# Two of eight depthwise convolution blocks on column strips of TensorE, and 64-partition transposes around the triangular inverses, in a one-layer RWKV-7 and Conformer trunk

## The chip, the core and the metric

The kernel runs on one core of one Trainium2 chip. The engines named below are those of the core: PE (TensorE, matrix products), DVE (VectorE), ACT (ScalarE), POOL (GpSimd) and SP (SyncE), which issues all DMA transfers of this kernel. PE reads its operands from SBUF, an on-chip memory of 128 partitions, and writes its results to banks of PSUM. Each engine executes its own instructions strictly in order, and waits at an instruction until the semaphores that it needs have been raised by other engines or by transfers.

The metric is the device time of one execution in microseconds (us): the median over several runs.

## The reference

One layer is computed for 1024 tokens of width 1024, in float32. A token mixer has two groups of channels that share an input projection and an output projection: an RWKV-7 recurrence with 8 heads of 64, and a causal depthwise convolution over 512 channels with 31 taps behind a gated unit. A feed-forward part with a small convolution follows.

```python
def _causal_dwconv(x, w, b):          # x: (B, T, C), w: (31, C)
    ...
    y = lax.conv_general_dilated(x, w[:, None, :], window_strides=(1,), padding=((K - 1, 0),),
                                 feature_group_count=x.shape[-1], ...)
    return y + b
...
def _wkv7(r, decay, k, v, a_vec, b_vec):
    def step(S, inp):
        sa = jnp.einsum("bhvk,bhk->bhv", S, a_t)
        S = S * w_t[:, :, None, :] + sa[..., None] * b_t[:, :, None, :] + v_t[..., None] * k_t[:, :, None, :]
        y = jnp.einsum("bhvk,bhk->bhv", S, r_t)
...
    c = u[..., :D_CONV] * jax.nn.sigmoid(u[..., D_CONV:])
    c = _causal_dwconv(c, cconv_w, cconv_b)
    c = jax.nn.silu(_layer_norm(c, cln_g, cln_b))
    mix = jnp.concatenate([rwkv_out, c], axis=-1) @ w_out
...
    x = x + _rms_norm(mix, norm_post_mix)
    f = _conv_ffn(_rms_norm(x, norm_pre_ffn), ffn_up, ffn_conv_w, ffn_conv_b, ffn_down)
    x = x + _rms_norm(f, norm_post_ffn)
```

The reference steps through the recurrence token by token. The kernel works it in chunks of 64 tokens, which needs, for each chunk and head, the inverse of a triangular 64x64 matrix.

## The kernel before

**Tiling.** The 1024 tokens are two halves of 512 (`h`), four quarters of 256 (`q`, two in each half), and sixteen chunks of 64 tokens, four in a quarter. A quarter thus has 4 chunks x 8 heads = 32 triangular matrices, held side by side. Channels lie in blocks of 128 on the partitions.

**Projections.** A weight tile is loaded by SP into `wr` (3 buffers, L159), split into a high and a low part (L153: the high part `wh` on ACT, the low part `wl` on POOL, 2 buffers each), and PE forms three products for each tile of the contraction into a PSUM bank `pb` (L126). This is so for the input projection `w_in`, for `w_out` and for the feed-forward part.

**The convolution group.** `glu_in` makes a tile `c` of 128 channels with 30 tokens of history ahead of 512 tokens. `conv` (L363 to L373) convolves it: one ACT instruction writes tap 0 and the bias into the PSUM bank `pc` (L370), and 30 dependent DVE instructions add the other taps (L373), the last of them into the SBUF tile `co`. There are four blocks of channels for each of two halves, so eight calls; they are written (half, block). The bank `pc` exists once and is shared with `conv_norm`, which normalizes the four `co` tiles of a half.

**The recurrence.** For a quarter, DVE and ACT work through elementwise decays, PE forms the scores (L473 to L498), and DVE scales them (`keys`, L500 to L520) into a tile `l` of 128 partitions x 32 matrices x 64 tokens. `inverses` (L532 to L551) then inverts the four 16x16 diagonal blocks of each of the 32 matrices by substitution: four transposes on DVE, each on 32 partitions (L539), bring them into the tile `dw`, and 14 pairs of small dependent DVE operations (`sub` at L549, `dw` at L551) work through the rows. `merge` (from L553) transposes the result back (two transposes at L561, four at L566, each on 32 partitions) and joins the 16x16 inverses into 64x64 ones by small products on PE (16 to 32 rows) with copies by ACT between them. The first PE instruction of a merge reads `dw`, so it is a good landmark: "merge q2" is the merge of quarter 2. After the merge the chunks of the quarter go through the recurrence proper in sequence (L643 to L686).

**What sets the order.** Every piece of work belongs to a stream ("first", "top", "rwkv", "norm", "conv", "proj"), and each stream has a number in the table `PRIO`. A scheduler takes these priorities, the dependencies and the buffers that are free, and writes out a fixed order for each engine ahead of time. The recurrence stands ahead of `norm`, `conv` and `proj`, which fill what it leaves. A call `conv(h, i, behind)` may only be scheduled behind a given instruction. In `mixer` (from L992) the calls (1,0) and (1,1) stand behind `sts[0]["normed"]` (the last instruction of the first half's `conv_norm`), (1,2) behind `W[3].mark` (the last transpose of quarter 3's merge), and (1,3) follows it. The order of the second half is: convolutions (1,0) and (1,1), output projection `w_out(0)` of the first half, quarter 3, `norm_ffn(0)`, convolutions (1,2) and (1,3), and then the feed-forward part.

Of the kernel before, what the change touches and what calls it, by code (L numbers as in the profile page):

```python
# [22 lines left out]
P = 128  # L23
# [13 lines left out]
CONV_W = 31  # L37
D_FF = 2816
# [8 lines left out]
BUFS = {"v": 2, "gd": 1, "pt": 6, "kk": 1, "l8": 5, "ca": 6, "ck": 6, "r": 2,  # L47
        "mixr": 1, "co": 4, "po": 1, "c": 4, "t2": 2}
EARLY, EVERY = 8, 3

# [41 lines left out]
class Trunk:  # L92
# [252 lines left out]
    def glu_in(self, h, hs, st, i):  # L345
# [3 lines left out]
        c = self.tl("c", [P, CONV_W - 1 + HALF])  # L349
        with self.tc.high_priority():  # L350
            nc.scalar.activation(c[:, CONV_W - 1:], ps2, AF.Tanh, scale=0.5)
# [5 lines left out]
        with self.tc.high_priority():  # L357
            nc.vector.scalar_tensor_tensor(c[:, CONV_W - 1:], c[:, CONV_W - 1:], 1.0, ps1, ALU.add, ALU.mult)
        if h == 0:
            nc.gpsimd.tensor_copy(self.ccarry[:, i], c[:, HALF:])  # L360
# [3 lines left out]
    def conv(self, st, i):  # L364
# [6 lines left out]
        for j in range(1, CONV_W):  # L371
            out = co if j == CONV_W - 1 else acc
            nc.vector.scalar_tensor_tensor(out, c[:, j:j + HALF], w(j), acc, ALU.mult, ALU.add)  # L373

# [125 lines left out]
    def keys(self, w):  # L500
# [14 lines left out]
        nc.gpsimd.memset(RT[32:64, :, 0:32], 0.0)  # L515
# [16 lines left out]
    def inverses(self, w):  # L532
# [3 lines left out]
        for g in range(2):  # L536
            for e in range(2):
                o = 16 * (1 - e)
                nc.vector.transpose(  # L539
                    self.dw[64 * e + 32 * g:64 * e + 32 * g + 32, o:o + 512].rearrange("p (i j) -> p i j", i=16),  # L540
                    Lq[64 + 32 * g:96 + 32 * g, :, 32 * g + 16 * e:32 * g + 16 * e + 16].rearrange("p u t -> p t u"))
# [11 lines left out]
    def merge(self, w):  # L553
# [5 lines left out]
        for g in range(2):  # L559
            gs = slice(32 * g, 32 * g + 32)  # L560
            nc.vector.transpose(up[gs].rearrange("p u j -> p j u"),  # L561
                                self.dw[gs, 16:1040].rearrange("p (i j) -> p j i", j=32)[:, 0:16])
            for e in range(2):
                o = 16 * (1 - e)
                c = 32 * g + 16 * e
                w.mark = nc.vector.transpose(  # L566
                    RT[gs, :, c:c + 16].rearrange("p u i -> p i u"),
                    self.dw[64 * e + 32 * g:64 * e + 32 * g + 32, o:o + 512].rearrange("p (i j) -> p i j", i=16))
# [378 lines left out]
    def mixer(self, sts):  # L947
# [60 lines left out]
        def conv(h, i, behind=None):  # L1008

            with ExitStack() as gate, self.stream("conv"):  # L1010
# [149 lines left out]
```

## Time and profile before

| | |
|---|---|
| median of 3 runs | 1372.5 us (1372.45 to 1373.0) |
| the profiled execution | 1373.94 us |
| its span in the profile | 1372.2 us |
| mean granted TensorE clock | 0.971 |
| instructions | 22752 |
| DVE busy in the span | 777.1 us |
| ACT busy in the span | 658.1 us |
| POOL busy in the span | 571.4 us |

The profile takes one execution apart. The execution lasted 1.7 us more than its span, which begins with the first instruction and ends with the last. "Busy" is the time in which an engine executes something. Consecutive matrix products overlap in PE, and the length that the profile gives to one is longer than the distance from one to the next, so a PE that is busy need not be at its peak. The chain of waits follows back from the last instruction to what released it at each step.

Some moments of this execution, each the start of an instruction in the timeline of PE, serve as landmarks below:

| landmark | us |
|---|---|
| merge q0 begins on PE | 139.8 |
| first score of quarter 2 | 343.2 |
| merge q2 begins on PE | 428.0 |
| first score of quarter 3 | 482.3 |
| merge q3 begins on PE | 523.9 |
| first product of the feed-forward part | 556.6 |

### The profile page before, as it was taken

Reading aid. Unit: us, or ns where it says so; the run is one execution under the profiler, and the core shown is the slowest. Engines: PE = TensorE matmul, PEld = TensorE weight load, DVE = VectorE, ACT = ScalarE, POOL = GpSimd, SP = SyncE. Lnnn points to the kernel's source line nnn. Section 1 sums busy time; section 2 is a strip of 40 time slices with the busy share of each in tenths; the row PEclk is TensorE's granted clock in tenths of the full one; section 3 lists DMA queues with packets and bytes.
Section 4 is the critical chain, followed back from the end, with each engine's and each line's share of the span. In section 5 each row is a group of like instructions: output and inputs, shape, how many; then the busy total and the mean of one; then the engine's idle time right before and its main releaser. Section 6 shows DMA issues by size and latency. Waiting matters only on the chain.

```text
span 1372.2 us, 22752 instructions
## 1 busy us (share of the span) xinstructions
PE 1299.9 (95%) x8688; PEld 1055.0 (77%) x8688; DVE 777.1 (57%) x1354; ACT 658.1 (48%) x1307; POOL 571.4 (42%) x496
## 2 busy tenths in 40 slices
PE   5999989999987996999999999999999999999998
PEld 4766767687776875878798888788888888888886
DVE  5367998997799969996315445500036654441002
ACT  6562553556645745647535555522244444443222
POOL 4443322243441331345444554444444544544443
PEclk9999889999998996999999999999999999999999
DMA  6222111121211423123345443443335443333333
GB/s 208 84 74 70 53 42 33 50 67 54 61 59 58 145 78 116 40 70 93 99 133 164 125 133 121 147 128 92 94 99 155 129 131 94 99 96 97 92 93 114
DMA packets 72252, 133.49 MB, mean 97 GB/s; under 512 B 7792, under 2 KB 14320, under 8 KB 72144
## 3 DMA queue, kind: packets, MB, share of 16 engines
q1 hardware_dynamic: 72144, 132.05, 32.6%
q8 instruction: 68, 1.11, 0.3%
q14 instruction: 40, 0.33, 0.1%
HBM read 119.43 MB, written 12.58 MB: 96 GB/s over the span
## 4 chain that ended last, share of the span: by engine, by line
PE 73%; DVE 18%; ACT 4%; issue 3%; DMA 1%; POOL 1%; SPq 0%; POOLq 0%; DVEq 0%; ACTq 0%
PE pb L126 65%; DVE pc L373 5%; PE pe L126 4%; PE xs L126 1%; DVE l L566 1%; DVE sub L549 1%; DVE dw L539 1%; DVE dw L551 1%; POOL wl L153 1%; DVE pt L442 1%; DVE l L506 1%; PE pe L141 1%; DVE dw L561 1%; PE Y L126 0%; DMA l<-x 0%
## 5 line engine op out<-in xcount | busy, mean ns | idle before, releaser
L153 POOL TENSOR_TENSOR wl<-wr,wh 128x512 fp32r<-128x512 f32 x376 | 495.1, 1318 | 622.5 <-ACT wh L153 599.7
L153 ACT CAST wh<-wr 128x512 fp32r<-128x512 f32 x376 | 231.5, 616 | 461.3 <-PE pb L126 263.3
L126 PE MATMUL pb<-f,wh 128*128 128x512 f32 x1408 | 436.9, 391 | 3.4 <-ACT pb L746 1.9
L126 PEld LDWEIGHTS pb<-f,wh 128*128 128x128 f32 x1408 | 264.0, 188 | 58.4 <-ACT pb L746 2.1
L126 PE MATMUL pb<-f,wl 128*128 128x512 f32 x704 | 276.4, 393 | 1.2 <-POOL wl L153 1.2
L126 PE MATMUL pb<-h,wh 128*128 128x512 f32 (+2 forms) x704 | 231.4, 407 | 2.6 <-ACT wh L153 2.3
L850 DVE SCALAR_TENSOR_TENSOR acc<-pb,params,acc 128x511 f32<-128x511 f32 (+1 forms) x144 | 107.5, 747 | 163.5 <-ACT acc L845 97.9
L373 DVE SCALAR_TENSOR_TENSOR pc<-c,params,pc 128x512 f32<-128x512 f32 x232 | 174.0, 750 | 6.5 <-ACT pc L370 3.1
L126 PEld LDWEIGHTS pb<-h,wh 128*128 128x128 f32 (+2 forms) x704 | 129.6, 188 | 37.0 <-ACT wh L153 4.4
L126 PEld LDWEIGHTS pb<-f,wl 128*128 128x128 f32 x704 | 132.4, 188 | 29.6 <-POOL wl L153 2.0
L126 PE MATMUL pb<-h,wl 128*128 128x512 f32 (+2 forms) x352 | 144.1, 409 | 2.5 <-POOL wl L153 2.5
L903 DVE TENSOR_TENSOR row<-pb,post_ffn 128x512 f32<-128x512 f32 x16 | 10.2, 685 | 209.2 <-ACT junk L902 209.2
L126 PE MATMUL pb<-wl,ahi 128*128 128x512 f32 x320 | 126.9, 397 | 0.1
L126 PE MATMUL pb<-wh,alo 128*128 128x512 f32 x320 | 126.2, 394 | 0.0
L126 PE MATMUL pb<-wh,ahi 128*128 128x512 f32 x320 | 88.6, 396 | 0.0
L126 PEld LDWEIGHTS pb<-h,wl 128*128 128x128 f32 (+2 forms) x352 | 66.0, 187 | 20.4 <-POOL wl L153 4.0
L126 PEld LDWEIGHTS pb<-wl,ahi 128*128 128x128 f32 x320 | 60.1, 188 | 14.9 <-POOL wl L153 0.6
L126 PEld LDWEIGHTS pb<-wh,alo 128*128 128x128 f32 x320 | 60.1, 188 | 14.4
L126 PEld LDWEIGHTS pb<-wh,ahi 128*128 128x128 f32 x320 | 59.7, 188 | 14.6
L126 PE MATMUL pb<-wh,m 128*128 128x256 f32 x256 | 52.5, 299 | 3.8 <-ACT m L153 2.9
L845 ACT ACTIVATE acc<-pb,params 128x512 f32<-128x512 f32 x72 | 55.7, 774 | 0.0
L153 DVE TENSOR_TENSOR alo<-acc,ahi 128x512 fp32r<-128x512 f32 x36 | 35.4, 983 | 24.9 <-ACT ahi L153 24.9
(248 smaller groups left out, 1807.8 us busy)
## 6 DMA issues: line engine op xcount, KB each, us to landing
wr<-ffn_up SPq DMA_DIRECT2D x176, 256.0 KB, 2.7
wr<-ffn_down SPq DMA_DIRECT2D x88, 256.0 KB, 2.7
wr<-w_in SPq DMA_DIRECT2D x80, 256.0 KB, 2.7
wr<-w_out SPq DMA_DIRECT2D x32, 256.0 KB, 2.7
mixd<-t SPq DMA_DIRECT2D x16, 256.0 KB, 3.1
nrow<-x1d SPq DMA_DIRECT2D x8, 512.0 KB, 4.2
out<-nrow SPq DMA_DIRECT2D x16, 256.0 KB, 2.4
l<-x SPq DMA_DIRECT2D x8, 256.0 KB, 5.7
```

Of the source, the lines that this page charges most:

```text
L126: return self.nc.tensor.matmul(out, lhsT, rhs, start=start, stop=stop, skip_group_check=skip)
L141: self.nc.tensor.transpose(out, in_, self.con("ident")[:n, :n])
L153: return self.nc.scalar.copy(hi, src), eng.tensor_tensor(lo, src, hi.bitcast(F32), ALU.subtract)
L373: nc.vector.scalar_tensor_tensor(out, c[:, j:j + HALF], w(j), acc, ALU.mult, ALU.add)
L442: nc.vector.tensor_tensor_scan(sg[:, l], self.con("scan"), sg[:, l], 0.0, ALU.mult, ALU.add)
L506: nc.vector.tensor_tensor(bv, bv, ge, ALU.mult)
L539: nc.vector.transpose(self.dw[64 * e + 32 * g:64 * e + 32 * g + 32, o:o + 512].rearrange("p (i j) -> p i j", i=16), Lq[64 + 32 * g:96 + 32 ...
L549: nc.vector.tensor_tensor(tv, dv[:, j + 1:, j:j + 1].broadcast_to([P, n, j]), dv[:, j:j + 1, :j].broadcast_to([P, n, j]), ALU.mult)
L551: nc.vector.tensor_tensor(dv[:, j + 1:, :j], dv[:, j + 1:, :j], tv, ALU.add)
L561: nc.vector.transpose(up[gs].rearrange("p u j -> p j u"), self.dw[gs, 16:1040].rearrange("p (i j) -> p j i", j=32)[:, 0:16])
L845: nc.scalar.activation(acc, ps, AF.Identity, scale=w(2), bias=self.par("fb", ch))
L850: nc.vector.scalar_tensor_tensor(acc[:, o:], ps[:, :HALF - o], w(j), acc[:, o:], ALU.mult, ALU.add)
```

## The change

The change has three parts; line numbers after it are higher by 4 (in the helpers at the top of the file) to 32 and more.

**Strips.** Convolutions (1,0) and (1,1) become `conv_strips`. `glu_in` writes the tile `c`, with two more columns of zeros, to a buffer `cd` in DRAM. `conv_strips` loads a tile of taps `cw` (128 x 1024 floats, from a new input that holds diagonal 32x32 blocks of taps), and for each of four blocks of 128 tokens reads `cd` back four times, shifted by 0 to 3 tokens, into `cs`: 4 shifts x 32 channels on the partitions, with the four groups of 32 channels side by side. Eight rounds of matmuls (4 taps each, 32 with one zero tap) then accumulate into `pc`; in a round four matmuls, one for each group of 32 channels, write 32 partitions each, from 32 columns of PE. That is 128 matmuls for a convolution, chained so that they keep their order. One ACT instruction writes `co`. `cs` and `cw` have one buffer each. `c` goes from 4 buffers to 2, and `ca` (masked scores of the recurrence) from 6 to 5.

**Transposes.** Two transposes on 64 partitions take the place of the four on 32 in `inverses`, three of the six in `merge`. A transpose moves blocks of 32x32, so some blocks must be moved along the free dimension besides: ACT copies one of 32x32x32 ahead of the first transposes and one behind the last, and a POOL memset of the tile `RT` moves from `keys` to behind the last transposes.

**Order.** (1,0) and (1,1) have no gate any more, (1,2) stands ahead of `w_out(0)` behind `W[2].mark`, and (1,3) stands behind `W[3].mark`.

```diff
@@ constants
-BUFS = {... "ca": 6, ... "c": 4, "t2": 2}
+BUFS = {... "ca": 5, ... "c": 2, "cs": 1, "cw": 1, "t2": 2}
+STRIPS = {(1, 0), (1, 1)}
@@ glu_in
+        if (h, i) in STRIPS:
+            nc.gpsimd.memset(c[:, -CPAD:], 0.0)
+            cd = self.dp.tile([P, CONV_W - 1 + HALF + CPAD], F32, name=self.nm("cd"))
+            nc.sync.dma_start(cd, c)
+            c = cd
         st["c", i] = c
@@ new, called in place of conv for (1, 0) and (1, 1)
+    def conv_strips(self, st, i):
+        nc = self.nc
+        cd, co, acc = st["c", i].rearrange("(q c) t -> c q t", q=4), self.tl("co", [P, HALF]), self.bank("pc")
+        st["co", i] = co
+        w = self.tl("cw", [P, ROUNDS, 4, 32])
+        nc.sync.dma_start(w, self.a["conv"][i])
+        m = 128
+        n = m + 4 * (ROUNDS - 1)
+        ins = []
+        for b in range(0, HALF, m):
+            cs = self.tl("cs", [P, 4, n])
+            for d in range(4):
+                nc.sync.dma_start(cs[32 * d:32 * d + 32], cd[:, :, b + d:b + d + n])
+            for r in range(ROUNDS):
+                for q in range(4):
+                    ins.append(self.mm(acc[32 * q:32 * q + 32, b:b + m], w[:, r, q], cs[:, q, 4 * r:4 * r + m],
+                                       start=r == 0, stop=r == ROUNDS - 1, skip=True))
+        self.chain(ins)
+        nc.scalar.activation(co, acc, AF.Identity, bias=self.par("cb", i), scale=0.5)
@@ keys
-        nc.gpsimd.memset(RT[32:64, :, 0:32], 0.0)
@@ inverses
-        for g in range(2):
-            for e in range(2):
-                o = 16 * (1 - e)
-                nc.vector.transpose(
-                    self.dw[64 * e + 32 * g:64 * e + 32 * g + 32, o:o + 512].rearrange(...),
-                    Lq[64 + 32 * g:96 + 32 * g, :, 32 * g + 16 * e:32 * g + 16 * e + 16].rearrange(...))
+        nc.scalar.copy(Lq[96:128, :, 0:32], Lq[96:128, :, 32:64])
+        for e in range(2):
+            o = 16 * (1 - e)
+            nc.vector.transpose(self.dw[64 * e:64 * e + 64, o:o + 512].rearrange(...),
+                                Lq[64:128, :, 16 * e:16 * e + 16].rearrange(...))
@@ merge
-        for g in range(2):
-            gs = slice(32 * g, 32 * g + 32)
-            nc.vector.transpose(up[gs]..., self.dw[gs, 16:1040]...)
-            for e in range(2):
-                ...
-                w.mark = nc.vector.transpose(RT[gs, :, c:c + 16]..., self.dw[64 * e + 32 * g:...]...)
+        nc.vector.transpose(up..., self.dw[0:64, 16:1040]...)
+        for e in range(2):
+            o = 16 * (1 - e)
+            w.mark = nc.vector.transpose(RT[0:64, :, 16 * e:16 * e + 16]..., self.dw[64 * e:64 * e + 64, o:o + 512]...)
+
+        nc.scalar.copy(RT[32:64, :, 32:64], RT[32:64, :, 0:32])
+        nc.gpsimd.memset(RT[32:64, :, 0:32], 0.0)
@@ mixer
-        conv(1, 0, sts[0]["normed"])
-        conv(1, 1, sts[0]["normed"])
+        conv(1, 0)
+        conv(1, 1)
+        conv(1, 2, W[2].mark)
         with self.stream("proj"):
             self.w_out(0, mixes[0], [sts[0]["co", i] for i in range(4)])
...
-        conv(1, 2, W[3].mark)
-        conv(1, 3)
+        conv(1, 3, W[3].mark)
         conv_norm(1)
```

Three places of the resulting order matter below. In these rows a number in a name counts the tiles, and "x4" is a run of four alike. The first place is DVE's queue from the transposes of quarter 2's inverses on; L539, L549 and L551 (before) and L572, L581 and L583 (after) are the transposes and the substitution, and L373 is a tap of convolution (1,0). Before:

```order
L539 STREAM_TRANSPOSE dw<-l_581_3597 32x512 x4
L309 SCALAR_TENSOR_TENSOR v_4318<-carry,params,v_4318 128x1
L313 SCALAR_TENSOR_TENSOR v_4318<-pb_4319,params,v_4318 128x511
L549 TENSOR_TENSOR sub_3758<-dw 128x14
L373 SCALAR_TENSOR_TENSOR pc_4530<-c_3264,params,pc_4530 128x512
L551 TENSOR_TENSOR dw<-dw,sub_3758 128x14
L373 SCALAR_TENSOR_TENSOR pc_4530<-c_3264,params,pc_4530 128x512
L549 TENSOR_TENSOR sub_3761<-dw 128x26
L373 SCALAR_TENSOR_TENSOR pc_4530<-c_3264,params,pc_4530 128x512
L551 TENSOR_TENSOR dw<-dw,sub_3761 128x13x2
```

And with the change:

```order
L572 STREAM_TRANSPOSE dw<-l_583_3597 64x512 x2
L581 TENSOR_TENSOR sub_3756<-dw 128x14
L583 TENSOR_TENSOR dw<-dw,sub_3756 128x14
L581 TENSOR_TENSOR sub_3759<-dw 128x26
L583 TENSOR_TENSOR dw<-dw,sub_3759 128x13x2
L581 TENSOR_TENSOR sub_3762<-dw 128x36
```

The taps between the steps of the substitution are gone from this stretch; they stand there no more because (1,0) is now PE's.

The second place is SP's queue where the strips are fed. L163 loads a weight tile, L399 is the four shifted reads of a block of 128 tokens, and L392 loads the taps of the second of the two convolutions; nothing like L399 and L392 was there before:

```order
L163 DMA wr_4496<-w_g 128x384
L399 DMA cs_4567<-cd_3300 32x4x156 x4
L163 DMA wr_4901<-w_out 128x512
L163 DMA wr_4931<-w_out 128x512
L399 DMA cs_4604<-cd_3300 32x4x156 x4
L163 DMA wr_4961<-w_out 128x512
L163 DMA wr_4991<-w_out 128x512
L399 DMA cs_4641<-cd_3300 32x4x156 x4
L163 DMA wr_5035<-w_out 128x512
L392 DMA cw_4681<-conv 128x1024
L399 DMA cs_4683<-cd_3381 32x4x156 x4
```

Each group of L399 has to wait until PE has read the block before it, since `cs` is one buffer, and weights stand behind it in the queue. In PE's queue a block of strips looks like this, between projections (`pb`), transposes (L145) and the gate (`gd`):

```order
L130 MATMUL pb_4477<-h_1849,wl_4481 96x512
L130 MATMUL pc_4527<-cs_4604,cw_4528 32x128 x9
L145 MATMUL pe_3925<-const,mixr_1915 128x128 x4
L130 MATMUL pe_3926<-gd_961,lora 128x128 x4
L145 MATMUL xs_93<-const,v_4396 64x128
L130 MATMUL pc_4527<-cs_4604,cw_4528 32x128 x23
L130 MATMUL pb_4477<-h_1851,wh_4498 96x512
```

The block's 32 matmuls stand close together, here in two pieces.

The third place is PE's queue around merge q3 (`pe<-dw,l` is the first product of the merge). Before:

```order
L126 MATMUL Y<-r_5437,ca_3643 64x64
L141 MATMUL xs_92<-const,v_4318 64x128 x2
L141 MATMUL xs_93<-const,v_4399 64x128 x2
L126 MATMUL pe_5495<-dw,l_793_5222 32x16 x64
L126 MATMUL pb_5912<-kk_5857,row_5864 128x128
L126 MATMUL pb_5921<-kk_5857,row_5864 128x128
```

And with the change:

```order
L130 MATMUL pb_5302<-wl_5366,m_4873 128x256
L130 MATMUL pb_5302<-wh_5365,m_4874 128x256
L130 MATMUL pb_5302<-wh_5365,m_4875 128x256
L130 MATMUL pb_5302<-wl_5366,m_4875 128x256
L130 MATMUL pe_5762<-dw,l_807_5492 32x16 x64
L130 MATMUL pb_5302<-wh_5365,m_4876 128x256
```

The products of `w_out(0)` (`pb<-wh,m` and `pb<-wl,m`), which had ended before this point, now stand on both sides of the merge, and the first products of `norm_ffn(0)` (`pb<-kk,row`), which stood right behind it, come later.

More of the change, by code (lines that the diff above doesn't have):

```diff
@@ L37 @@
 CONV_W = 31
+ROUNDS = 8
+CPAD = 2
 D_FF = 2816
@@ L348, in glu_in @@
         ps2 = self.project(a["w_in"][16 + i], P, hs)
[L349 removed]
+        c = self.tl("c", [P, CONV_W - 1 + HALF + CPAD])
         with self.tc.high_priority():
[L351 removed]
+            nc.scalar.activation(c[:, CONV_W - 1:-CPAD], ps2, AF.Tanh, scale=0.5)
         ps1 = self.project(a["w_in"][12 + i], P, hs)
@@ L357, in glu_in @@
         with self.tc.high_priority():
-            nc.vector.scalar_tensor_tensor(c[:, CONV_W - 1:], c[:, CONV_W - 1:], 1.0, ps1, ALU.add, ALU.mult)
+            u = c[:, CONV_W - 1:-CPAD]
+            nc.vector.scalar_tensor_tensor(u, u, 1.0, ps1, ALU.add, ALU.mult)
         if h == 0:
-            nc.gpsimd.tensor_copy(self.ccarry[:, i], c[:, HALF:])
+            nc.gpsimd.tensor_copy(self.ccarry[:, i], c[:, HALF:-CPAD])
+        if (h, i) in STRIPS:
[3 more added lines that the diff above has]
+            c = cd
         st["c", i] = c
@@ L558, in merge @@
         up = self.dw[64:128, 528:1040].rearrange("p (u j) -> p u j", j=16)
-        for g in range(2):
-            gs = slice(32 * g, 32 * g + 32)
-            nc.vector.transpose(up[gs].rearrange("p u j -> p j u"),
-                                self.dw[gs, 16:1040].rearrange("p (i j) -> p j i", j=32)[:, 0:16])
-            for e in range(2):
[L564 to L568, printed above, removed]
+        nc.vector.transpose(up.rearrange("p u j -> p j u"),
+                            self.dw[0:64, 16:1040].rearrange("p (i j) -> p j i", j=32)[:, 0:16])
+        for e in range(2):
+            o = 16 * (1 - e)
+            w.mark = nc.vector.transpose(
+                RT[0:64, :, 16 * e:16 * e + 16].rearrange("p u i -> p i u"),
+                self.dw[64 * e:64 * e + 64, o:o + 512].rearrange("p (i j) -> p i j", i=16))
+        nc.scalar.copy(RT[32:64, :, 32:64], RT[32:64, :, 0:32])
+        nc.gpsimd.memset(RT[32:64, :, 0:32], 0.0)
         yield
@@ L1010, in conv @@
             with ExitStack() as gate, self.stream("conv"):
+                if (h, i) in STRIPS:
+                    self.conv_strips(sts[h], i)
+                    return
                 if behind is not None:
@@ L1140, in pack @@
         np.concatenate([vals[n].reshape(c, P) for n, c in PARAMS]).T)
+    cw = np.zeros((4 * ROUNDS, 4, 4, 32), np.float32)
+    cw[:CONV_W] = f("cconv_w")[0].reshape(CONV_W, 4, 4, 32)
+    taps = np.zeros((4, 4, 32, ROUNDS, 4, 32), np.float32)
+    ch = np.arange(32)
+    taps[:, :, ch, :, :, ch] = cw.reshape(ROUNDS, 4, 4, 4, 32).transpose(4, 2, 1, 0, 3)
+    out["conv"] = taps.reshape(4, P, ROUNDS, 4, 32)
     out["consts"] = constants()
```

8 lines of the change are left out of this document (4 added, 4 removed).

## The prediction

> **What bounds the kernel now.** I read the page's busy times first, then its forty slices, then the chain of waits.
>
> ```profile
> span 1372.2 us, 22752 instructions
> PE 1299.9 (95%) x8688; PEld 1055.0 (77%) x8688; DVE 777.1 (57%) x1354; ACT 658.1 (48%) x1307; POOL 571.4 (42%) x496
> PE   5999989999987996999999999999999999999998
> DVE  5367998997799969996315445500036654441002
> PEclk9999889999998996999999999999999999999999
> PE 73%; DVE 18%; ACT 4%; issue 3%; DMA 1%; POOL 1%; SPq 0%; POOLq 0%; DVEq 0%; ACTq 0%
> ```
>
> PE is busy almost always, but the slices split the span in two: up to the sixteenth (some 550 us) DVE is as full as PE and the clock dips, behind it PE alone is full. The chain agrees: 18% of it is DVE, all in the first part. One piece of it shows what a full PE is:
>
> ```profile
> 896.31 463.55 PE pb L126 x2016
> ```
>
> Here 2016 products of 512 columns take 463.55 us, 0.230 each, without a gap. In this second part only PE's work counts. In the first part each stage has its own limit, so I cut it at the landmarks of the table above (columns: stage, its length, then busy us and instructions of PE, weight loads, DVE, ACT, POOL, then granted clock, DMA share, GB/s), and set the taps of the convolution on DVE (L373) beside it:
>
> ```profile
> 343.00:428.00 85.00, 75.14 (x466) 59.25 (x466) 75.10 (x145) 44.63 (x93) 32.80 (x29) 0.94 0.19 55
> 428.00:482.00 54.00, 49.34 (x780) 43.80 (x779) 49.73 (x73) 36.20 (x85) 14.87 (x14) 0.91 0.41 123
> 482.00:524.00 42.00, 33.79 (x385) 27.21 (x383) 31.03 (x75) 19.44 (x49) 13.19 (x15) 0.95 0.31 89
> 524.00:557.00 33.00, 27.02 (x530) 24.58 (x529) 30.74 (x57) 18.36 (x44) 2.27 (x4) 0.65 0.24 82
> 557.00:1372.00 815.00, 801.14 (x3932) 661.11 (x3930) 324.04 (x543) 355.57 (x678) 385.44 (x303) 1.00 0.38 111
> ```
>
> ```profile
> 343.00:428.00 85.00, 20.90 (x28) 0.94 0.19 55
> 428.00:482.00 54.00, 23.55 (x32) 0.91 0.41 123
> 482.00:524.00 42.00, 0.36 (x1) 0.95 0.31 89
> ```
>
> Between 343 and 482 us DVE is busy for nine tenths of the time, and almost a third of that is taps. Where they lie is seen on DVE's timeline in quarter 2's substitution:
>
> ```profile
> 384.01 1.05 DVE L549 TENSOR_TENSOR sub<-dw 128x14 f32<-128x14 f32 x1
> 384.99 0.74 DVE L373 SCALAR_TENSOR_TENSOR pc<-c,params,pc 128x512 f32<-128x512 f32 x1
> 385.64 0.67 DVE L551 TENSOR_TENSOR dw<-dw,sub 128x14 f32<-128x14 f32 x1
> 386.23 0.74 DVE L373 SCALAR_TENSOR_TENSOR pc<-c,params,pc 128x512 f32<-128x512 f32 x1
> 386.89 0.17 DVE L549 TENSOR_TENSOR sub<-dw 128x26 f32<-128x26 f32 x1
> 387.01 0.76 DVE L373 SCALAR_TENSOR_TENSOR pc<-c,params,pc 128x512 f32<-128x512 f32 x1
> ```
>
> Each step of 0.2 us carries a tap of 0.75 behind it, in order, so the substitution that the whole second half waits for takes over 40 us. Quarter 3's, which has no tap in it (the row of 482 to 524 has one), ended within its stage of 42 us.
>
> **What the strips cost PE.** No row shows four strips of 32 columns. Two of 64 columns are shown (start, length):
>
> ```profile
> 462.98 0.22 PE L126 MATMUL xs<-r,ck 128*64 128x64 f32 x1
> 462.99 0.22 PE L126 MATMUL Y<-r,ca 128*64 128x64 f32 x1
> 463.04 0.22 PE L126 MATMUL xs<-r,ck 128*64 128x64 f32 x1
> 463.05 0.22 PE L126 MATMUL Y<-r,ca 128*64 128x64 f32 x1
> 410.58 1.06 PE L126 MATMUL pe<-gd,lora 96*128 96x128 f32 x8
> ```
>
> Both strips of a pair start within 0.01 us, and the next pair follows after 0.06: they run side by side. The last row has float32 products of 128 columns, two records to a product: with 0.28 for the last one, (1.06 - 0.28) / 7 = 0.11 us per record. The 256 strip products make 512 records; four abreast that is 128 x 0.11 = 14 us for both convolutions, one after another 512 x 0.11 = 56. I take 14, since the pair shows it, and keep 56 for a rival. The run is broken some 20 times by other work. What a change of tiling costs:
>
> ```profile
> 500.72 0.28 PE L126 MATMUL Y<-r,l 64*64 64x64 f32 x2
> 500.92 0.39 PE L126 MATMUL pb<-wh,m 128*128 128x256 f32 x1
> ```
>
> The second of the pair of records starts near 500.78, the full-width product 0.14 later instead of 0.06: about 0.1 us for a change, 40 changes some 3 us, inside the rounding of the sum. The Trainium skill, "TensorEngine Tiling (Array Packing)", section Tiling Modes, states that "Changing tiling mode (not just tile) drains the TensorE"; the trace agrees at 0.1 us each. By the record's whole length of 0.28 for a drain, the sum would be 11 us and not 3.
>
> **What DVE and ACT gain and pay.** The strips take 60 taps from DVE (0.75 us each, and the timeline's distances are 0.66 where two follow): 40 to 45 us. The transposes, by the groups of instructions:
>
> ```profile
> L539 DVE STREAM_TRANSPOSE dw<-l 32x512 f32<-32x512 f32 x16 | 17.3, 1084 | 0.3
> L566 DVE STREAM_TRANSPOSE l<-dw 32x512 f32<-32x512 f32 x16 | 16.8, 1049 | 0.3
> L561 DVE STREAM_TRANSPOSE dw<-dw 32x512 f32<-32x512 f32 x8 | 8.8, 1105 | 0.3
> L609 ACT COPY l<-l 64x512 f32<-64x512 f32 x16 | 9.9, 617 | 4.8 <-PE pe L126 4.5
> L424 ACT ACTIVATE kk<-kk 128x1024 f32<-128x1024 f32 x4 | 4.2, 1058 | 8.3 <-DVE kk L422 8.3
> ```
>
> A quarter loses two at L539, one at L561 and two at L566: 2.17 + 1.1 + 2.1 = 5.4 us, if a transpose of 64 partitions takes what one of 32 does (each partition has 512 elements as before). The bound on the other side is twice as long, which saves nothing. I take the first, since the elements per partition stay the same. Each quarter gains two ACT copies of 1024 elements per partition: between 0.62 and 1.06 us by the last two rows. The one ahead of the transposes is on the path, with a handover on each side; the one behind them is followed by the merge, whose first products read `dw`, not `RT`. The moved memset runs on an idle POOL. That leaves 3.5 us per quarter, with 5 and -1 as ends. `ca` with 5 buffers can hold up the last mask of a quarter until the recurrence of the quarter before has read its own; I cost it at nothing, because that recurrence is over before the substitution begins, and at 2 us where it isn't.
>
> **The sum, by stages.** The matmuls between landmarks are counted in the order, at 0.230 us for 512 columns, and 0.12 for 256 columns, from these rows:
>
> ```profile
> 423.41 0.40 PE L126 MATMUL pb<-wh,m 128*128 128x256 f32 x2
> 423.65 0.28 PE L126 MATMUL pb<-wl,m 128*128 128x256 f32 x1
> ```
>
> - *Up to 343:* transposes of quarters 0 and 1, 2 x 3.5: **-7** (+2 to -10).
> - *343 to 428:* PE loses 48 products of 512 columns and 74 of 256, which go later (11.0 + 8.9), and gets four strip blocks (7): -13. DVE loses 20.9 of taps and 5.4 of transposes: -26. Both were about equally full, so PE is the one late next: **-12** (0 to -25).
> - *428 to 482:* PE loses 78 products of 256 columns (9.4) and gets the other strips (7). DVE loses 23.6 of taps and gets some 20 of convolution (1,2), 14 us: -9. Part of this becomes PE's wait for strips: **-6** (+8 to -12).
> - *482 to 524:* PE gets 127 products of `w_out(0)` more, 15 us, on 26.5 that I count there: 41.7 in a stage of 42. DVE gets some 10 taps (7) and loses 5.4. The stage grows: **+5** (0 to +12).
> - *524 to 557:* PE gets 15 us more here, on 14 (the rest of `w_out(0)` and the last chunks of quarter 2). In this stage PE waits for DVE and the clock is 0.65, so some of it fits: **+10** (0 to +20).
> - *From 557:* the same work no longer stands here: PE's count falls by **-12** (-5 to -15), where the clock is 1.00 and nothing hides it.
>
> The sum is -22. As a check: from 343 to 557 the order's counts give PE 148 us of work in 214 before, 162 after, and the sum makes that stretch 211 long: what PE doesn't fill falls from 66 to 49 us, which one interleaved substitution of 40 us on DVE makes believable. The profiled execution took 1373.9 us, 1.4 above the median of the runs; 1373.9 - 22 = 1352 is 1350.5 beside the median, so I say 1350.
>
> **Rivals.** 0.2%, 2.7 us, is what a measurement of this kernel can tell from no change.
>
> *Strips starved through DRAM (slower).* `cs` has one buffer: SP can start the next four reads only when PE has finished a block, and PE's queue is strictly in order, so a late block stops everything. The nearest landings:
>
> ```profile
> po<-post_mix SPq DMA_DIRECT2D x8, 128.0 KB, 4.2
> row<-x SPq DMA_DIRECT2D x4, 512.0 KB, 4.0
> 525.00:550.00 25.00, 19.88 (x383) 18.41 (x384) 24.16 (x47) 12.74 (x30) 2.27 (x4) 0.57 0.29 102
> ```
>
> With four issues in a row a block lands some 5.5 us after the one before it was read. It decides from the point where PE's other work between two blocks is less; the order has 2.7 to 7 us there. For it: at two or three of the seven gaps the work is under 5.5, the last read of a block stands behind a `row` load that waits for DVE, and a PE that waits lowers its clock (the window's row has 0.57, behind gaps of some 3 us). Against: most gaps have the work. If six of seven stall by 6 us: +36 on -22, **1386**. The Trainium skill, "TensorE: Matmul & The Clock Gate", Part 1, has the clock halved after one idle window of about 3.4 us; the trace agrees with its 0.57, and each such stall would then slow the next microseconds too.
>
> *The gain is given back around merge q3.* `w_out(0)` was PE's filler before the merge and now lies on both sides of it, and the feed-forward part must wait for `norm_ffn(0)`, which waits for it. If those two stages take +12 and +20 instead of +5 and +10, and 428 to 482 gives -3, the sum is -2: **1370**. For it: the count of 41.7 in 42 us; against: those two stages had 34 us that PE didn't fill (75 long, 40.5 of work).
>
> *Strips one after another.* If four strips of 32 columns don't run abreast as two of 64 do, PE gets 42 us more; 15 of it may fall in unfilled time: **1377**. The pair of rows speaks against it.
>
> *More gain.* If the substitution of quarter 2 takes the 15 us that its steps need, the stage ends at DVE's -25, and with no growth at merge q3: **1325**.
>
> **How the numbers follow.** Forecast (1330 to 1364) 0.71; more gain 0.05; given back 0.08, half of it within 0.2%; starved 0.12; serial strips 0.04. Faster by over 0.2% is 0.71 + 0.05 + 0.04 = 0.80; the same 0.05, with a corner of the starved case; slower 0.15. The range from 1328 to 1372 leaves out the slower cases and a corner of the fast one. The bounds of the stages added up would be wider, but they exclude each other: what one gains another fills.
>
> **What would show it.** In the profile after: strip records in fours within 0.05 us, 0.11 from four to four, or else serial; transposes of 64x512 at 1.1 us or at 2.2; merge q0 at 136 and merge q2 at about 409 instead of 428, with no tap between its substitution's steps; first score of quarter 3 near 457, merge q3 near 504, first feed-forward product near 547. Idle PE ahead of `cs` products, released by DMA, would mean the strips starve. The forecast is wrong if stalls there add up to more than 20 us, or if the feed-forward part starts later than 565.

## The result and the profile after

The changed kernel takes 1383.65 us (median of 5 runs, 1383.02 to 1385.43), the kernel before 1372.5 us beside it (1371.89 to 1374.63): ratio 1.0081, with a 95% interval of 1.0067 to 1.0094. It is slower by 11 us where 22 us less were forecast. The profiled execution of the changed kernel took 1383.09 us, its span 1381.0 us. The stages below compare the two profiled executions, whose spans differ by 8.8 us and not by 11, because the one of the kernel before lay 1.4 us above its median.

These are the page's busy times and slices after:

```profile
span 1381.0 us, 23784 instructions
PE 1309.3 (95%) x9200; PEld 1063.3 (77%) x9200; DVE 723.6 (52%) x1274; ACT 668.6 (48%) x1316; POOL 569.5 (41%) x498
PE   6999869999898997999999999999999999999998
DVE  5367985887686699864215444500036654441002
PEclk9999978999999997899999999999999999999999
```

DVE is busy for some 53 us less, PE for 9 us more, and the time is longer. The clock is not the reason: its mean is 0.977, before 0.971. The landmarks show where the time went. Each is the start of an instruction on PE's timeline, and the two columns on the right give the change of the stage that ends there, in us:

| landmark | before | after | stage: forecast | stage: measured |
|---|---|---|---|---|
| merge q0 | 139.8 | 134.8 | | |
| first score of quarter 1 | 201.9 | 210.6 | | |
| merge q1 | 250.8 | 267.8 | | |
| first score of quarter 2 | 343.2 | 357.8 | -7 | +14.6 |
| merge q2 | 428.0 | 425.1 | -12 | -17.5 |
| first score of quarter 3 | 482.3 | 475.3 | -6 | -4.2 |
| merge q3 | 523.9 | 524.2 | +5 | +7.4 |
| first feed-forward product | 556.6 | 578.1 | +10 | +21.2 |
| end of the span | 1372.2 | 1381.0 | -12 | -12.7 |

With the old transposes only 2 of the 128 records of a merge stand at its landmark in quarters 1 to 3; the others follow 1 to 3 us later, so a comparison of merges is exact to no more than that.

Two stages carry the error: the first (22 us away from its forecast), in which the forecast saw only transposes, and the one behind merge q3 (11 us). The feed-forward part starts later than 565, which the prediction had named as a sign that it is wrong. The waits from 150 to 215 us, as a list of engine, line, what it waited for, total, times and longest, name what is new in the first:

```profile
ACT c L355 <- DVE co L383: 15.6, 2, 12.8
```

ACT's and PE's timelines show the same wait from both sides (start, length, instruction, and in brackets the idle time before it and its releaser):

```profile
205.34 0.60 ACT L355 ACTIVATE c<-pb 128x512 f32<-128x512 f32 x1 [12.78 <-DVE co L383]
```

```profile
194.20 0.42 PE L145 MATMUL pe<-const,co 128*128 128x128 f32 x1
206.00 0.69 PE L145 MATMUL pb<-const,mixr 128*128 128x128 f32 x2 [11.38 <-ACT c L355]
```

And this is what DVE did meanwhile:

```profile
193.49 11.04 DVE L383 SCALAR_TENSOR_TENSOR pc<-c,params,pc 128x512 f32<-128x512 f32 x14
204.56 0.75 DVE L383 SCALAR_TENSOR_TENSOR co<-c,params,pc 128x512 f32<-128x512 f32 x1
```

L355 is in `glu_in`, here of the first half's fourth block: ACT is to write another tile `c`, but `c` now has two buffers instead of four, and both hold blocks whose taps DVE has not finished. ACT stands at that instruction until the last tap (`co`) has read its tile. (The third block waited for 2.8 us in the same way.) The transposes of quarter 1's input need the same `pb` banks, whose next reader is that ACT instruction, so PE stands too. In the trace of before, no wait of ACT at a tile `c` is among its longest waits there.

The strips themselves did what the sum said. Their group, and one stretch of 48 records from the timeline:

```profile
L130 PE MATMUL pc<-cs,cw 128*32 128x128 f32 x512 | 19.3, 276 | 1.2 <-DMA cs<-cd 1.2
```

```profile
420.13 1.52 PE L130 MATMUL pc<-cs,cw 128*32 128x128 f32 x48 [1.19 <-DMA cs<-cd]
```

48 records, twelve times four abreast, take 1.52 us, of which the last four are 0.28 long: (1.52 - 0.28) / 11 = 0.11 from four to four. 512 records make 128 steps of 0.11, 14 us, and the only wait of PE for `cs` in the list is the 1.19 us in the brackets. The transposes and the copies, with mean ns behind the comma:

```profile
L572 DVE STREAM_TRANSPOSE dw<-l 64x512 f32<-64x512 f32 x8 | 8.7, 1093 | 0.7 <-ACT l L569 0.6
L595 DVE STREAM_TRANSPOSE l<-dw 64x512 f32<-64x512 f32 x8 | 8.6, 1074 | 0.1
L569 ACT COPY l<-l 32x1024 f32<-32x1024 f32 x4 | 4.2, 1044 | 5.3 <-DVE l L530 5.2
```

A transpose of 64 partitions takes what one of 32 took, 1.09 us, and the copy is at the upper end of its bounds.

Quarter 2's substitution became short as well, and that did not bring its merge forward as much. These are its first and last step, the transpose behind it, and the first products of the merge on PE:

```profile
399.27 0.18 DVE L581 TENSOR_TENSOR sub<-dw 128x14 f32<-128x14 f32 x1
408.40 0.17 DVE L583 TENSOR_TENSOR dw<-dw,sub 128x14 f32<-128x14 f32 x1
408.68 1.15 DVE L591 STREAM_TRANSPOSE dw<-dw 64x512 f32<-64x512 f32 x1
425.08 2.20 PE L130 MATMUL pe<-dw,l 32*32 32x16 f32 x128
```

The substitution took 9 us, where it took 42 before (384.0 to 425.6). But the merge's products began 15 us behind the end of the transpose at L591. PE was busy for 13.4 of the 15 us between 410 and 425: strips, input projections and the gate stood ahead of the merge in its queue. In the kernel before, the merge followed DVE at once:

```profile
426.37 1.15 DVE L561 STREAM_TRANSPOSE dw<-dw 32x512 f32<-32x512 f32 x1
427.96 0.23 PE L126 MATMUL pe<-dw,l 32*32 32x16 f32 x2
```

So the prediction's step "PE is the one late next" is what happened in this stage. With strips and full buffers (a kernel of the next section) the transpose ended at 375.8 and the merge began at 396.7; without strips the merge followed its transpose within 0.1 us.

### The profile page after: what moved, and what is told of

The parts are those of the page before. It is cut to its first block, busy times and chain, and to the rows that moved or that the text cites. A ratio compares the mean times of both kernels' runs of the same rounds, so it can differ in the third digit from the quotient of the medians.

```text
span 1381.0 us, 23784 instructions
## 1 busy us (share of the span) xinstructions
PE 1309.3 (95%) x9200; PEld 1063.3 (77%) x9200; DVE 723.6 (52%) x1274; ACT 668.6 (48%) x1316; POOL 569.5 (41%) x498
## 4 chain that ended last, share of the span: by engine, by line
PE 52%; issue 1%; ACT 1%; POOL 1%; DVE 0%; POOLq 0%; DVEq 0%
PE pb L130 52%; POOL wl L157 1%; ACT pb L778 0%; PE pn L145 0%; DVE t L772 0%; ACT wh L157 0%; ACT mixr L745 0%; DVE nrow L918 0%; ACT junk L934 0%; ACT co L427 0%; DVE row L935 0%; ACT pt L877 0%; DVEq L1192 0%; POOLq L1192 0%; POOL ss L152 0%
## 5 line engine op out<-in xcount | busy, mean ns | idle before, releaser
L383 DVE SCALAR_TENSOR_TENSOR pc<-c,params,pc 128x512 f32<-128x512 f32 x174 | 130.9, 752 | 9.4 <-ACT pc L380 5.7
L130 PEld LDWEIGHTS pb<-wh,alo 128*128 128x128 f32 x320 | 60.1, 188 | 14.3
L882 DVE SCALAR_TENSOR_TENSOR pt<-pb,params,pt 128x511 f32<-128x511 f32 (+1 forms) x32 | 23.9, 747 | 47.1 <-ACT ecarry L879 46.7
```

The lines of the kernel that those rows point to most:

```text
L130: return self.nc.tensor.matmul(out, lhsT, rhs, start=start, stop=stop, skip_group_check=skip)
L882: nc.vector.scalar_tensor_tensor(acc[:, o:], ps[:, :HALF - o], w(j), acc[:, o:], ALU.mult, ALU.add)
```

## The experiments

The theories: **A**, the two buffers of `c` cost the first half its time; **B**, the fifth `ca` buffer does; **C**, `w_out(0)` ends late behind the strips; **D**, PE's total work and what it can't fill set the second half, so that DVE time saved there is worth little, against **E**, the prediction's stages. Others (F to K) are named in the expectations that they belong to. All ratios are to the kernel before, run on the same chip, with 95% intervals. The scheduler writes the order anew for each kernel, so a small edit can move instructions far away; the landmarks are read beside each time for that reason.

**One buffer of `ca` less, alone.** `"ca": 6` becomes `"ca": 5` in the kernel before.

> The kernel before with 5 buffers for ca instead of 6, nothing else changed. Theory A (the first half lost its time because the tile c has 2 buffers): this stays within 2 us of before, 1371 to 1375. Theory B (the first half lost it because the last mask of a quarter waits for the fifth ca buffer): the stretch from the first score of quarter 1 to its merge grows from 48.9 us towards the 57.3 of the change, and the time is some 8 us longer, 1380.

1369.95 us, ratio 0.9987 (0.9977 to 0.9996). The stretch from quarter 1's first score to its merge grew from 48.9 to 57.5 us, as B says (200.4 to 257.9), but quarter 2's first score came at 343.7, against 343.2 before, and the time was not longer. The wait is real and here costs nothing.

**The transposes alone.** `inverses`, `merge` and the memset as changed, in the kernel before.

> The kernel before with the 64-partition transposes, the two ACT copies and the moved memset, nothing else. By the sum of the prediction four quarters give 3.5 us each, of which all four lie on the path: 1358 to 1362. A rival: in quarters 1 to 3 the transposes stand beside taps and projections that take the same time anyway, and only quarter 0 shows it: 1367 to 1371. If the copy ahead of the transposes costs more than it saves: 1374 or more.

1369.26 us, 0.9978 (0.9965 to 0.9991). The landmarks moved far more than the time: quarter 2's first score 10 us earlier (333.1), merge q3 27 us earlier (497.2), and then the first feed-forward product 5 us later (561.9). The rival's range holds, for another reason than it gave: the gain was there at merge q3 and was given back behind it.

**Four tiles `c` again in the first half.** The memory of `cw` and `cs` is not used before quarter 2, so blocks 2 and 3 of the first half go there:

```diff
-        c = self.tl("c", [P, CONV_W - 1 + HALF + CPAD])
+        spare = {(0, 2): ("cw", [P, 2 * HALF]), (0, 3): ("cs", [P, 624])}.get((h, i))
+        c = self.tl(*spare)[:, :CONV_W - 1 + HALF + CPAD] if spare else self.tl("c", [P, CONV_W - 1 + HALF + CPAD])
```

> The changed kernel, but the tiles c of the first half's blocks 2 and 3 are put into the memory of cw and cs, which are not used before quarter 2, so that the first half has four tiles c again; all else as changed. Theory A (c has 2 buffers): ACT's wait of 12.8 us at the third tile c goes, the first score of quarter 1 comes at 197 to 200 us instead of 210.6, and the end moves with it: 1368 to 1373. Theory B (ca): the first score of quarter 1 moves as well, but quarter 1's merge still comes 57 us after it. Theory C (what decides is that w_out(0) ends late, before merge q3 and the feed-forward part): the gain of the first half is lost again before the feed-forward part, and the time is 1379 to 1384.

1366.45 us, 0.9960 (0.9945 to 0.9975), against 1.0081 with two buffers: some 17 us. ACT's wait at `c` is gone from the same list of waits, whose longest is now an ordinary one:

```profile
ACT pt L479 <- DVE pt L476: 5.4, 2, 3.5
ACT pc L381 <- DVE co L384: 4.0, 1, 4.0
```

Quarter 1's first score came at 195.1 (210.6 with two buffers), quarter 2's at 343.8 (357.8). The later landmarks then stood near the forecast's: merge q2 at 406.7 (forecast 409), quarter 3's first score at 456.5 (457), merge q3 at 505.5 (504), but the first feed-forward product at 558.0 (547). A's mechanism holds, 2 us below its range; B's part holds too, since quarter 1's merge still came 61 us behind its first score. C alone does not, since the gain reached the end. The landmarks from quarter 2 on stood 14 to 20 us earlier, and the first of these follows from the wait; how much of the 17 us at the end is due to the new order is not separated.

**The strips behind `w_out(0)`.** From that kernel, the calls for (1,0) and (1,1) move behind `w_out(0)`, into its stream:

```diff
-        conv(1, 0)
-        conv(1, 1)
         conv(1, 2, W[2].mark)
         with self.stream("proj"):
             self.w_out(0, mixes[0], [sts[0]["co", i] for i in range(4)])
+        with self.stream("proj"):
+            self.conv_strips(sts[1], 0)
+            self.conv_strips(sts[1], 1)
```

> As the kernel with c in the memory of cw and cs, and the strips of (1,0) and (1,1) issued after w_out(0), with its priority, so that w_out(0) isn't behind them. Theory C (w_out(0) behind the strips holds up the feed-forward part): the last tile of w_out(0) comes more than 10 us earlier relative to merge q2, the feed-forward part starts some 33 to 40 us behind merge q3 instead of 54, and the time is 8 to 12 us below that kernel's. Theory A alone: the same time as that kernel within 4 us, because PE has the same work to do before the feed-forward part ends either way.

1371.99 us, 0.9999 (0.9988 to 1.0009). The last result of `w_out(0)` did not come earlier (518.9, against 516.6), and the feed-forward part began 58 us behind merge q3. The time is 5 us longer than that kernel's, outside the ranges of C and of A. Three quarters of the strip records now ran behind `w_out(0)`, so the strips alone are not what keeps it late.

**The change without strips.** `STRIPS = set()`, four buffers `c`, six `ca`; transposes and order as changed.

> The changed kernel without strips: (1,0) and (1,1) stay on DVE as 30 taps each, without a gate, c has 4 buffers and ca 6; transposes and order as changed. Theory D (the second half is set by PE's total work and by what PE can't fill, so DVE time saved there is worth little, while the strips' 14 us on PE are paid): about 1364 to 1370, the same as with strips and four tiles c (1366.5) within 4 us. Theory E (the prediction's: the taps in quarter 2's substitution hold up everything behind, and freeing DVE is worth 18 us in the stages of quarter 2): 1378 to 1385, with quarter 2's merge at 425 or later.

1363.91 us, 0.9928 (0.9913 to 0.9943): faster than with strips, though 60 taps are back on DVE. Merge q2 stands at 403.7, not at 425: E's numbers fall, and D's number holds. DVE's timeline still had the taps between the steps of quarter 2's substitution, and it took 34 us; it merely began earlier (367 instead of 384). This kernel has six `ca` as well, so the strips are not all that sets it apart from the one with four tiles `c`; two later runs take that apart.

**Strips with the old transposes.** The kernel with four tiles `c`, with `inverses`, `merge` and the memset of before.

> The kernel with strips and c in the memory of cw and cs, but with the transposes of before on 32 partitions. Theory D: the transposes are worth here about what they were worth on the kernel before (3 us of 1372), so 1368 to 1371. Theory E (they lie on the path in all four quarters): 1378 to 1381.

1374.48 us, 1.0007 (0.9994 to 1.0020). The transposes are worth 6 to 8 us here, between the two expectations, and no theory gave that.

**All four blocks of the second half as strips.** `STRIPS` holds (1,0) to (1,3).

> The kernel with c in the memory of cw and cs, with all four blocks of the second half as strips: 14 us more on PE, 45 us less on DVE. Theory D: PE's work is paid, DVE's is not gained: 1374 to 1384. Theory E: the stages around merge q3, where the taps of (1,2) and (1,3) lie, get shorter by some 15 us: 1352 to 1364.

1386.83 us, 1.0105 (1.0084 to 1.0127). D's direction, and 3 us beyond its range. On the page PE is busy for 1323.3 us instead of the 1304.8 of the kernel with two strips and four tiles `c`, and idle for 61 us instead of 59: PE's work is paid, and nothing is gained. Merge q3 came at 492.2, the earliest yet, and the feed-forward part only at 594.3, 102 us later: `w_out(0)` ended at 557.8.

**Six buffers `ca` beside the strips.** Room is made by one buffer of `t2` instead of two.

> The kernel with c in the memory of cw and cs, with 6 buffers for ca again, and t2 with one buffer instead of two to make room. Theory B (the fifth ca buffer costs the stretch from quarter 1's first score to its merge): that stretch falls from 60.7 us to about 50. By theory D the end moves by less, since the kernel before with 5 buffers was no longer than with 6: 1362 to 1368.

1374.57 us, 1.0011 (1.0001 to 1.0020). The first half did as B says (quarter 1's merge 49.2 us behind its first score, quarter 2's first score at 333.0 instead of 343.8), but the time is some 7 us longer than with five `ca` and two `t2`, not shorter. The room taken from `t2` is a likely reason, not tested alone: PE's waits for the banks that ACT gives back in `w_out` (L779) were 3.4 us, four times, in that kernel, and are here 11.2 us, eight times:

```profile
PE pb L130 <- ACT pb L779: 11.2, 8, 4.7
```

**The fifth `ca` buffer, without strips.** As the kernel without strips, with `"ca": 5`.

> The kernel without strips and with four buffers c (transposes and order as changed), but with 5 buffers for ca instead of 6. Beside the kernel with strips and four tiles c, which also has 5, this is the price of the strips alone. Theory B (the fifth ca buffer takes back what the transposes bring to the first half): quarter 2's first score at 343 to 345 instead of 332.8, and 1366 to 1374. Theory D without B (it is made up for by what PE fills, as on the kernel before): 1362 to 1366.

1372.50 us, 1.0002 (0.9992 to 1.0011), against 0.9928 with six: 9 us. Quarter 2's first score came at 344.4, against 332.8. DVE's timeline shows where the mask went. With six buffers:

```profile
225.73 0.41 DVE L530 TENSOR_TENSOR l<-pe,const 128x256 f32<-128x256 f32 x1
226.06 0.41 DVE L531 TENSOR_TENSOR ca<-pe,const 128x256 f32<-128x256 f32 x1
```

and with five:

```profile
225.27 0.74 DVE L530 TENSOR_TENSOR l<-pe,const 128x256 f32<-128x256 f32 x2
237.60 0.76 DVE L531 TENSOR_TENSOR ca<-pe,const 128x256 f32<-128x256 f32 x2
```

The last mask of quarter 1 (L531) is written 11.5 us later. DVE does not stand still meanwhile: the order has put the mask into the substitution, behind the point where a chunk of quarter 0 has read the tile. PE's timeline has that read, 3 us ahead of the mask:

```profile
234.56 0.22 PE L130 MATMUL Y<-r,ca 128*64 128x64 f32 x1
```

Until then the scores wait in PSUM banks `pe`, and merge q1, which needs them, came at 256.4 instead of 245.4. On the kernel before the same wait cost nothing: with the old transposes quarter 2 started at 343 either way. Here it takes back the 10 us that the new transposes bring there.

**A quarter of the strips.** From the kernel with four tiles `c`:

```diff
-            for r in range(ROUNDS):
+            for r in range(2):
```

> The kernel with strips and c in the memory of cw and cs, with only 2 of the 8 rounds of strips (24 of the 31 taps are left out): 10.5 us less on PE, nothing else less. Theory D (PE's work is paid in full): 1354 to 1358, 8 to 12 us below 1366.5. A rival F (the strips lie in time that PE couldn't fill anyway, and the end is set by the chain of recurrence, w_out(0) and norm_ffn): within 4 us of 1366.5.

1373.78 us, 1.0005 (0.9996 to 1.0015): 7 us longer, though 10 us of products are left out. Neither D nor F gives this. The order came out different: PE waited 10.4 us in all for `mixr` at L737, against 0.3 us with all eight rounds. As a test of D this run decides nothing; it shows what another order can cost.

**Full buffers and strips.** The last masked scores of quarter 1 go into what `c` leaves of `cw`, so the first half has six `ca` and four `c`. To make room, the pool of small tiles goes from 4 buffers to 2:

```diff
+        if (h, i) == (0, 2):
+            self.last_ca = c[:, 544:1056].rearrange("p (h t) -> p h t", h=NH)
...
-            CA = self.tl("ca", [P, NH, CH])
+            CA = self.last_ca if len(w.CA) == 3 and w.q == 1 else self.tl("ca", [P, NH, CH])
```

> The kernel with strips and c in the memory of cw and cs, with the last masked scores of quarter 1 put into what is left of cw, so that the first half has six buffers for ca as well (the rotating small tiles have 2 buffers instead of 4 to make room for 128 bytes). Theory G (buffers: two of c and one of ca were the price of the strips' memory, and without it strips are worth some 6 us): quarter 1's merge some 49 us behind its first score, quarter 2's first score at 332 to 335 instead of 343.8, and the time 1355 to 1361. Rival H (the strips are worth nothing, since PE has to do their 14 us): the first half as in G, and the time that of the kernel without strips, 1364, or more, up to 1369.

1362.88 us, 0.9934 (0.9916 to 0.9951): nearer to H. The first half is as G says (quarter 2's first score at 331.3), but the time is that of the kernel without strips (0.9928), 2 us above G's range and 1 us below H's. Taken together, the two intervals leave room for some 2 us in favour of the strips, and not for G's 6. What the two small buffers cost was not measured alone. With these buffers equal, the strips bring merge q2 7 us forward (396.7 against 403.7) and merge q3 12 us (500.5 against 512.4), and the feed-forward part starts 13 us later (560.4 against 547.2).

**The order alone.** The kernel before with the new calls of the four convolutions.

> The kernel before with only the calls of the four convolutions in the new order (no gate for (1,0) and (1,1), (1,2) behind quarter 2's last transpose, (1,3) behind quarter 3's), everything else as before. From the kernel without strips (0.9928) and the one with the transposes alone (0.9978), the order is worth 0.5%: 1364 to 1369. If the order is worth something only together with the earlier merges of the new transposes: 1371 to 1375.

1385.71 us, 1.0097 (1.0080 to 1.0114), in neither range. Merge q3 came at 540.9, 17 us later than before. The same calls that stand in the kernel without strips, which is 10 us faster than the kernel before, make it 13 us slower with the old transposes. The parts of this change do not add.

**`w_out(0)` ahead of the convolutions.** From the kernel with full buffers:

```diff
-        with self.stream("proj"):
+        with self.stream("norm"):
             self.w_out(0, mixes[0], [sts[0]["co", i] for i in range(4)])
```

> The kernel with strips and full buffers in the first half (1362.9), with w_out(0) at the priority of the norms instead of the projections, so ahead of the convolutions and strips. Theory J (the feed-forward part starts 41 to 47 us after the last result of w_out(0), which is late because it fills PE behind everything else): that result comes 8 us or more before 515, the feed-forward part starts before 552, and the time is 1352 to 1359. Theory D (PE's total work and what the recurrence leaves unfilled set the end; a filler used earlier is missing later): w_out(0) ends earlier, and the time is within 4 us of 1362.9 or longer.

1360.77 us, 0.9921 (0.9904 to 0.9938). J's mechanism is there: the last result of `w_out(0)` came at 503.5 instead of 515.1, the feed-forward part began at 546.7 instead of 560.4, 43 us behind it. But the time is D's: 2 us, inside both intervals, for a start 14 us earlier. Of the kernels that compute everything it has the lowest median.

**DVE's taps behind merge q3.** From the kernel with full buffers, 29 taps of (1,3) are left out:

```diff
-        for j in range(1, CONV_W):
+        for j in (CONV_W - 1,) if short else range(1, CONV_W):
```

> The kernel with strips and full buffers in the first half, with 29 of the 30 taps of (1,3) left out, the ones that DVE works between merge q3 and the feed-forward part: 22 us less on DVE there, nothing less on PE. Theory K (DVE's queue is what makes that stretch 60 us long): the feed-forward part starts 10 us or more earlier, below 550, and the time is 1350 to 1357. Theory D (PE's filler is used up by then and the recurrence's round trips are what is left): the stretch shortens by less than 5 us, and the time stays within 4 us of 1362.9.

1357.62 us, 0.9895 (0.9881 to 0.9910). The feed-forward part began at 556.0, 4 us earlier, as D says, and the time is 5 us shorter for 22 us less of DVE, between the two ranges.

## Why the prediction was wrong

**The step that failed is the first term, "Up to 343", at -7; it was +14.6.** It took up the transposes and nothing else.

- *`c` with two buffers was listed as part of the change and never costed.* The sum followed the convolutions of the second half, where the strips free `c` at once, and not those of the first, where every block is still convolved by taps and a tile is held for as long as they last. It cost 14 us at quarter 2's first score and 17 at the end, by the kernel that gives the tiles back. The 14 follow the wait in the trace; the 17 hold what the new order does as well.
- *`ca` with five buffers was costed at nothing, "because that recurrence is over before the substitution begins", and at 2 us where it isn't.* It isn't, in the first half: 11.6 us at quarter 2's first score. As a time this is 9 us with the new transposes, and none with the old ones.
- *The transposes themselves* were worth 10 us there (333.1 against 343.2), where -7 was said. The three together, 14 + 11.6 - 10, come to +16 beside the +14.6 measured.

**The second step that failed is +10 for the stage from merge q3 to the feed-forward part; it was +21.** The rival "The gain is given back around merge q3" had the place and nearly the sizes of these stages: -3, +12 and +20 where -4.2, +7.4 and +21.2 were measured. It missed the time because it shared the first term. The last result of `w_out(0)` (the DVE instruction that takes it out of PSUM) came at 534.4 instead of 509.7, while merge q3 stayed where it was. Over the sixteen kernels the feed-forward part begins 36 to 54 us behind that result (before 46.9, after 43.7, with four tiles `c` 41.4), but anywhere from 18 to 102 us behind merge q3. What these some 45 us are made of was not taken apart.

**Where the sum was right.** Strips abreast, 14 us; no starvation (1.2 us where the rival had 36); transposes at 1.09; "From 557" -12.7 for -12; and 343 to 524 together -14.3 for -13, with -17.5 and +7.4 for -12 and +5 inside. With `c` repaired, merge q3 stood within 2 us of the forecast, and that is luck: the first stage was 8 us too long (343.8 for 336) and the next one 10 us shorter than its forecast (63 us for 73). One price does not follow from its terms: "More gain", with -7, -25, -6, 0, 0 and -12, makes -50 and so 1322, not 1325.

**Was the forecast's reason right at all?** For the landmarks up to merge q3, in part; for the time, no. Repaired in both buffers, the strips are worth nothing that these runs can measure (0.9934 with them, 0.9928 without); with five `ca` on both sides they are worth 6 us (0.9960 and 1.0002). The pages without strips and with strips and full buffers, in this order, show why:

```profile
span 1362.2 us, 22740 instructions
PE 1292.0 (95%) x8688; PEld 1051.9 (77%) x8688; DVE 759.1 (56%) x1334; ACT 665.8 (49%) x1315; POOL 568.9 (42%) x496
span 1360.5 us, 23796 instructions
PE 1300.5 (96%) x9200; PEld 1057.9 (78%) x9200; DVE 718.5 (53%) x1274; ACT 658.4 (48%) x1310; POOL 570.0 (42%) x498
```

With strips PE is idle (span less busy time) for 10 us less, 60.0 instead of 70.2, and busy for 8.5 us more. With five `ca` it is idle for 20 us less (59.2 instead of 79.1) and busy for 14 more. So PE waited less where DVE was freed, and PE's own longer work took most or all of it back. The windows show where. Without strips, from quarter 3's first score on:

```profile
460.00:512.00 52.00, 42.14 (x469) 36.90 (x467) 49.73 (x103) 23.57 (x56) 14.69 (x16) 0.95 0.29 89
512.00:547.00 35.00, 31.07 (x563) 27.91 (x563) 29.45 (x60) 21.97 (x51) 4.93 (x8) 0.59 0.30 104
547.00:1362.00 815.00, 800.50 (x3899) 660.48 (x3898) 306.09 (x510) 352.99 (x672) 384.43 (x302) 1.00 0.39 111
```

With strips and full buffers:

```profile
445.00:500.00 55.00, 50.41 (x553) 44.86 (x546) 49.24 (x99) 23.32 (x55) 14.22 (x16) 0.97 0.24 72
500.00:560.00 60.00, 49.39 (x847) 43.83 (x846) 52.06 (x102) 40.15 (x101) 19.41 (x20) 0.80 0.30 96
560.00:1360.00 800.00, 787.14 (x3678) 650.60 (x3676) 281.74 (x472) 332.78 (x634) 376.50 (x294) 0.99 0.38 113
```

Behind merge q3 there are 847 records on PE instead of 563, and behind the start of the feed-forward part 221 fewer, 15 us less. The feed-forward stage has little slack (PE is busy for 98% of it), so its length is PE's work: what was done ahead of it is saved there, and most of what the strips brought forward had only moved. The prediction counted both halves of this (+10 and -12) and yet took the gains ahead of merge q3 as won. That PE's total work is what pays fits this, the kernel with four blocks as strips and the one with `w_out(0)` ahead; it is not proved, since the one run that took PE work away came out longer, with another order. How much of each difference of 5 to 10 us belongs to the order remains open.

For the measured +11: from the kernel without strips (0.9928), the fifth `ca` buffer gives +0.74%, the strips -0.42%, and the two buffers of `c` +1.21%, which is the 1.0081 measured. The steps lead from one kernel to the next, so they add up whatever their causes are. The middle step compares kernels with different orders, and with six buffers it is nothing.

## What to carry to other kernels

When a change takes memory, cost every buffer that it gives up where that tile lives longest, which may be far from the place that the change is about; an in-order engine that waits for such a buffer holds everything behind it. Where the work behind a point is bound by one engine, a gain ahead of that point counts only if that engine does less in all or waits less in all: look for what fills it later, not for the stage that got shorter. And with an order that a scheduler writes anew, compare landmarks and waits before the end times, and don't add up parts that were measured one by one.

## What the runs showed of the hardware

- Four float32 strips of 32 columns and 128 rows ran abreast at 0.11 us per step of 128 columns, the same as one record of a product 128 columns wide (0.11 in the kernel before). That is four times as fast as one after another at 0.11 each. The Trainium skill, "TensorE: Matmul & The Clock Gate", Part 3, gives a speedup of 2.38 for three column tiles at 512 columns; the trace here has more, with four.
- The reads of `cs` from DRAM landed 2.2 us after their issue, each of 78 KB by the profile. The prediction took 4.2 us for the nearest row and some 5.5 for a block of four; the weight loads of the kernel before, 256 KB in 2.7 us, were nearer. The load of `cw` took 5.3:

```profile
cs<-cd SPq DMA_DIRECT2D x32, 78.0 KB, 2.2
cw<-conv SPq DMA_DIRECT2D x2, 512.0 KB, 5.3
```

- An ACT copy of 32 partitions x 1024 elements took 1.04 us, as an activation of 128 x 1024 did in the kernel before (1.06): the number of partitions made no difference there, as for DVE's transposes of 32 and 64 partitions.
